# Second pair of delta-rule heads begun from keys and queries alone, values projected later

## The chip, the core and the metric

The kernel runs on one core of one Trainium2 chip and computes the whole model in one launch. The metric is the device time of one execution in microseconds, the median of several. TensorE (PE) multiplies matrices into PSUM; VectorE (DVE), ScalarE (ACT) and GpSimd (POOL) work beside it; SyncE (SP), ACT and POOL issue DMAs. Each engine runs its own instructions strictly in the order in which the program lists them and waits on semaphores for the others.

## The reference

Two residual layers on 512 tokens of width 1024, in float32. The even layer (the one that the change touches) projects the normed input h once and splits the columns: group A, four heads of a gated delta rule with short convolutions, and group B, four heads of differential attention. Both outputs go through one output projection. The odd layer is a forgetting attention. After each mixer follow a squared-ReLU MLP and a gated per-layer embedding. Of group A:

```python
qkv_a, z_a, b_a, a_a, q_b, k_b, v_b = split_cols(h @ w_in, EVEN_SPLITS)
qkv_a = silu(causal_conv(qkv_a, conv_w))           # width 4, per column
q_a, k_a = l2_norm(q_a), l2_norm(k_a);  beta = sigmoid(b_a);  g = -exp(a_log) * softplus(a_a + dt_bias)
# per head and chunk:
a_mat = tril(beta k k^T * decay, -1) + I           # needs keys, beta and g, no values
u, w  = solve(a_mat, [beta v, beta k exp(gc)])     # values enter only here
v_new = u - w S;  o = q_dec S + qk v_new;  S = S * g_last + k_dec^T v_new   # chunk after chunk
```

## The kernel before, in words

Every large product is made of three float32r products (high and low parts of weight and activation), so a weight half of 128 x 1024 is loaded by SP (`raw`), its high part is made by ACT and its low part by DVE (`whl`, three buffers, lines 146 and 149).

The even mixer is written as Python generators. A list of projections, `fill`, taken in the order of the string `ORDER` (line 72), gives TensorE its large products: `a0` to `a3` project one delta head's query and key columns each, `w0` and `w2` the values of two delta heads, `v0` and `v1` the values of the attention heads, `b0` to `b3` one attention head's query and key, and two more jobs project the gate z. Between them, `chains` (lines 676 and on) advance the heads themselves: each `yield n` says how much later on TensorE's own count of columns the next step may be written. What has been written is then ordered again per engine by the framework's scheduler, so that the place of an instruction follows from its estimate of when the inputs are there. On the chip that place is fixed.

A delta head (`gdn_head`, line 453) runs in these steps: the decays `et` from the gates (`decays`); key products `pg` and turned keys; a small column `lc` of each 16 x 16 diagonal block; the query-key product; squares of the keys `sqk` and queries `sqq`; the turned values `vb`. When both heads of a pair have their `lc`, `small_inverses` writes it to DRAM (`lsc`), copies it back to the rows of all blocks (`lb`) with DMAs issued by ACT, and makes 15 pairs of small steps on POOL (`xt`, `xc`, lines 446 and 448). Then POOL spreads the result to `x` (line 535), TensorE turns it to `z`, and three levels of products (`ub`, `yy`) build the inverse of each 128 x 128 block. At last comes the recurrence over four chunks: `rest`, `vn`, `state`, `u`, and a norm of the output (`sqo`, `sso`, `ro`, line 648).

Heads 0 and 1 are the first pair, 2 and 3 the second (`ABREAST` is 2). Heads 2 and 3 enter `gdn_head` at once but stay in its first loop (lines 454 and 455) until an earlier head is done and their values are projected:

```python
while len(done) < h + 1 - ABREAST or h >= ABREAST and h not in vts:
    yield 2.0
```

Tiles come from pools with a fixed number of buffers: `sp` (10) holds et, kd, u, x and z of the heads, `hl` (8) the split queries, keys and outputs and the attention values, `mm` (3) PSUM sums of projections, `ax` small PSUM products, `raw` and `whl` (3 each) the weights.

Of the kernel before, what the change touches and what calls it, by code (L numbers as in the profile page):

```python
# [10 lines left out]
F32 = mybir.dt.float32  # L11
F32R = mybir.dt.float32r
I32 = mybir.dt.int32
AF = mybir.ActivationFunctionType
ALU = mybir.AluOpType
# [3 lines left out]
P = 128  # L19
T = 512  # L20
NT = T // P
# [3 lines left out]
HA = 4  # L25
# [11 lines left out]
BASE = 16  # L37
# [31 lines left out]
LAT_A, LAT_B = 1.55, 1.7  # L69
W_G, W_B, W_T, W_V, W_Q = 10.0, 22.5, 20.0, 6.0, 3.6  # L70
Z_B, DSTEP = 3, 3.47
ORDER = "a0 a1 w0 v0 v1 b0 b1 a2 a3 w2 b2 b3"
ABREAST = 2
N_SP = 10
N_ST = 5
SRAW, SWHL, SA = 8, 3, 4
ORDER_MID, ORDER_END = (1, 5, 6, 7, 3, 4, 2), (1, 2, 5, 6, 3, 7, 4)
# [20 lines left out]
def trunk(ctx: ExitStack, tc: tile.TileContext, I, cst, out):  # L98
    nc = tc.nc
    V, S, G, PE = nc.vector, nc.scalar, nc.gpsimd, Tensor(tc)  # L100
# [13 lines left out]
    def aux():  # L114
        return pax.tile([P, T], F32, tag="ax", name="ax", bufs=2)
# [8 lines left out]
    def hl32():  # L124

        return hlp.tile([P, 2, T], F32, tag="hl", name="hl32")
# [12 lines left out]
    def v3(ap):  # L139
        return ap.rearrange("p (i c) -> p i c", c=P)  # L140
# [23 lines left out]
    ident, m_le, m_gt = (gen[:, j * P:(j + 1) * P] for j in range(3))  # L164
# [22 lines left out]
    def wsplit(raw, E=None):  # L187

        n = raw.shape[2]
        w = tile_of(whp, F32R, "whl", 2)[:, 0:8 * n].rearrange("p (j k c) -> p j k c", j=2, c=n)  # L190
        split(w[:, 0], w[:, 1], raw, E)
        return w

    def wload(src, spans, r0=0):
        return [wsplit(wraw(src, spans, r0 + half * 4 * P)) for half in range(2)]
# [126 lines left out]
    def even_mixer(act, first, wba):  # L322
        w_in = I["w_in_even"][0]
        with ExitStack() as es:
            gp = es.enter_context(tc.tile_pool(name="gp", bufs=1))
            def sp(name):
                return gp.tile([P, T], F32, tag="sp", name=name, bufs=N_SP)

            def st_(name):
                return gp.tile([P, T], F32, tag="st", name=name, bufs=N_ST)  # L330
# [66 lines left out]
            def conv_tile(ps, j, name):  # L397

                y = gp.tile([P, T], F32, tag="qkv", name=name, bufs=12)
                w = [cols[:, R_CONV + 12 * a + j:R_CONV + 12 * a + j + 1] for a in range(4)]  # L400
                S.activation(out=y, in_=ps, func=AF.Copy, scale=w[3])
                for a in (2, 1, 0):
                    d = 3 - a
                    V.scalar_tensor_tensor(out=y[:, d:], in0=ps[:, :T - d], scalar=w[a], in1=y[:, d:],
                                           op0=ALU.mult, op1=ALU.add)
                return y

            def silu(*tiles):
                for y in tiles:
                    S.activation(out=y, in_=y, func=AF.Silu)  # L410

            def hcol(name, h):
                return st[name][:, :, h]

            def bc(ap):
                return ap.broadcast_to([P, NT, P])
# [16 lines left out]
            def small_inverses(pair):  # L433

                lc, n = small_l[pair], 2 * NT
                lsc = dp.tile([P // BASE, BASE * n * BASE], F32, tag="lsc", name="lsc", bufs=1)
                nc.scalar.dma_start(lsc.rearrange("b (r n) -> b r n", r=BASE), lc.rearrange("p h i c -> p (h i c)"))
                lb = gp.tile([P, BASE, n, BASE], F32, tag="lb", name="lb", bufs=1)
                for a in range(P // BASE):
                    nc.scalar.dma_start(lb[a * BASE:(a + 1) * BASE].rearrange("p r i c -> p (r i c)"),  # L440
                                        lsc[a:a + 1, :].broadcast_to([BASE, BASE * n * BASE]))
                yield 10.0
                xc = small_w[pair].rearrange("p h i c -> p (h i) c")
                tmp = gp.tile([P, n, BASE], F32, tag="xt", name="xt", bufs=1)
                for c in range(BASE - 1, 0, -1):
                    G.tensor_tensor(out=tmp[:, :, 0:c], in0=lb[:, c, :, 0:c],
                                      in1=xc[:, :, c].broadcast_to([P, n, c]), op=ALU.mult)
                    G.tensor_tensor(out=xc[:, :, 0:c], in0=xc[:, :, 0:c], in1=tmp[:, :, 0:c], op=ALU.add)
                yield 10.0
                solved.append(pair)  # L450

            def gdn_head(h, qT, kT):
                while len(done) < h + 1 - ABREAST or h >= ABREAST and h not in vts:
                    yield 2.0
                if h >= ABREAST:
                    yield from decays(h)
                blk = [slice(i * P, (i + 1) * P) for i in range(NT)]

                pair, sub = h // 2, h % 2
# [3 lines left out]
                pk = aux()  # L463
                for i in range(NT):
                    PE.transpose(pk[:, blk[i]], kT[:, blk[i]], ident)
                sq, kk = st_("sqk"), gp.tile([P, 2, NT], F32, tag="kk", name="kk", bufs=ABREAST)
                for i in range(NT):
                    S.activation(out=sq[:, blk[i]], in_=pk[:, blk[i]], func=AF.Square, accum_out=kk[:, 0, i:i + 1])
                kd = sp("kd")
                S.activation(out=kd, in_=pk, func=AF.Copy)  # L470
                dg = st_("dg")
                V.tensor_tensor(out=v3(dg), in0=v3(pg), in1=mid(gm["minus_base"]), op=ALU.mult)
                second = pair in small_l
# [5 lines left out]
                while h not in decay or "ec" not in st:  # L479
# [13 lines left out]
                                in1=s.broadcast_to([P, NT, BASE]), op=ALU.mult)  # L493
# [9 lines left out]
                                op=ALU.mult)  # L503
# [4 lines left out]
                for i in range(NT):  # L508
                    PE.matmul(pq[:, blk[i]], lhsT=kT[:, blk[i]], rhs=qT[:, blk[i]], start=True, stop=True)
                V.tensor_tensor(out=et, in0=pq, in1=et, op=ALU.mult)  # L510
                G.tensor_tensor(out=v3(kd), in0=v3(kd), in1=bc(hcol("ekd", h)), op=ALU.mult)

                pq = aux()
                for i in range(NT):
# [1 line left out]
                sq, eq = st_("sqq"), kk[:, 1]  # L516
# [6 lines left out]
                vT = vts[h][0]  # L523
# [4 lines left out]
                V.tensor_tensor(out=v3(vb), in0=v3(pv), in1=bc(n2), op=ALU.mult)  # L528
                yield 2.0

                while pair not in solved:
                    yield 1.0
                x, xc = sp("x"), small_w[pair][:, sub]
                for i in range(NT):
                    G.tensor_tensor(out=x[:, blk[i]].rearrange("p (b c) -> p b c", c=BASE),
                                    in0=xc[:, i, :].unsqueeze(1).broadcast_to([P, P // BASE, BASE]),
                                    in1=gm["minus_base"].rearrange("p (b c) -> p b c", c=BASE), op=ALU.mult)
# [13 lines left out]
                for lv in LEVELS:  # L551
                    y, wide, full = st_("yy"), lv < 32, lv == P // 2
                    ub = u
                    if not full:
# [5 lines left out]
                        else:  # L560
                            for j in range(64 // lv):
                                c = slice((2 * j + 1) * lv, (2 * j + 2) * lv)
                                G.tensor_tensor(out=cut(ub, lv)[:, j::64 // lv], in0=v3(u)[:, :, c],
                                                in1=mu[:, c].unsqueeze(1).broadcast_to([P, NT, lv]), op=ALU.mult)
# [11 lines left out]
                    else:  # L576
                        for j in range(64 // lv):
                            S.activation(out=y[(2 * j + 1) * lv:(2 * j + 2) * lv, 0:T // 2],
                                         in_=py[j * lv:j * lv + lv, 0:T // 2], func=AF.Copy)
# [8 lines left out]
                    else:  # L588
                        for j in range(64 // lv):
                            zo = half(z[2 * j * lv:(2 * j + 1) * lv], lv, 1)[:, j::64 // lv]  # L590
                            V.tensor_tensor(out=zo, in0=zo, in1=cut(pt[j * lv:j * lv + lv], lv)[:, j::64 // lv],
                                            op=ALU.subtract)
# [11 lines left out]
                for n in range(NT):  # L604
                    vn = gp.tile([P, P], F32, tag="vn", name="vn", bufs=2 * ABREAST)
                    if n:
# [4 lines left out]
                                               in1=vb[:, blk[n]], op0=ALU.mult, op1=ALU.subtract)  # L611
# [7 lines left out]
                    if n < NT - 1:  # L619
                        ps = aux()  # L620
# [21 lines left out]
                sq = st_("sqo")  # L642
# [21 lines left out]
            def project_a(h):  # L664
                c = h * P
                tiles = []
                w = wload(w_in, [(C_Q + c, P), (C_K + c, P)]) if h else first
                pair = [acc(), acc()]
                steps = [gemm_steps(pair[m], w, m, act) for m in range(2)]
                if h == 0:  # L670
                    for _ in zip(*steps):
                        yield
                for m, ps in enumerate(pair):
                    yield from steps[m]
                    tiles.append(conv_tile(ps, 4 * m + h, "qk"[m] + "T"))
                    if h < ABREAST:
                        silu(tiles[-1])
                heads_a.append(tiles[0])
                late.extend(tiles if h >= ABREAST else [])
                spawn(gdn_head(h, *tiles), W_G)  # L680

            def values_a(h):
                w = wload(w_in, [(C_V + h * P, 2 * P)])
                for m in range(2):
                    ps = acc()
                    yield from gemm_steps(ps, w, m, act)
                    late.append(conv_tile(ps, 8 + h + m, "vT"))
                silu(*late)
                for m in range(2):
                    vts[h + m] = late[m - 2], PE.time + W_V * LAT_A  # L690
                late.clear()

            def project_b(h):
                c = h * P
# [54 lines left out]
            def spawn(g, after, lat=LAT_A):  # L749
                chains.append([PE.time + after * lat, g, lat])  # L750
# [3 lines left out]
            late, small_l, small_w, solved = [], {}, {}, []  # L754
            chains, done, done_b, started, heads_a, heads_o = [], [], [], [], [], [None] * (HA + HB)
            qks, vts, decay = {}, {}, {}
# [17 lines left out]
            while chains or fill:  # L774
                due = [c for c in chains if c[0] <= PE.time]
                free = [f for f in fill if f[0]()]
                if due:
                    c = min(due, key=lambda c: c[0])
# [615 lines left out]
    with tc.tile_pool(name="ip", bufs=1) as ip:  # L1394
# [18 lines left out]
        ps = acc()  # L1413
# [3 lines left out]
        for i in range(NT):  # L1417
# [3 lines left out]
            r, ok, ss = small(1, "rx"), small(1, "ok"), ssx[:, i:i + 1]  # L1421
# [6 lines left out]
            if i == 2:  # L1428
                ps = acc()
# [9 lines left out]
        act, _ = new_act()  # L1439
# [61 lines left out]
```

## Time and profile before

| | us |
|---|---|
| median of 3 runs | 1422.2 (1421.55 to 1423.59) |
| the profiled execution | 1421.96 |
| its span, first to last instruction | 1420.2 |
| TensorE busy / DVE / ACT / POOL | 1384.1 / 867.3 / 773.5 / 174.2 |
| mean granted TensorE clock | 0.989 |

The profile shows one execution. A line of a timeline gives the start, the busy time, the engine, the source line, the operation, output and inputs, the count and, in brackets, how long the engine was idle before and what ended that. PEclk is the share of the full TensorE clock that was granted. In groups, the busy time of a product can overlap the next one's, so what one costs is read from a run of them: so many products from one start to the next. The mixer covers about 20 to 322 us of the span.

### The profile page before, as it was taken

How to read it: one execution, taken by the hardware profiler on the slowest of the kernel's cores; microseconds unless marked ns; L12 is line 12 of the kernel's file. 1: busy time of each engine (PE TensorE's matmuls, PEld its weight loads, DVE VectorE, ACT ScalarE, POOL GpSimd, SP SyncE). 2: the span in 40 equal slices, each digit the busy share in tenths (PEclk: the TensorE clock that was granted, in tenths of full speed). 3: DMA queues.
4: the chain of work that ended last, by engine and by line, in shares of the span. 5: the costliest groups of instructions: out<-in, count | busy, mean ns of one | idle time of the engine just before them, and what ended most of it. 6: DMA issues, size and time to landing. Idle time of an engine off the chain costs nothing. (4 is left out here: it accounts for less than half of the span.)

```text
span 1420.2 us, 18495 instructions
## 1 busy us (share of the span) xinstructions
PE 1384.1 (97%) x6969; PEld 1152.2 (81%) x6969; DVE 867.3 (61%) x1535; ACT 773.5 (54%) x1304; POOL 174.2 (12%) x231
## 2 busy tenths in 40 slices
PE   8999987999999999999999999999999999999997
PEld 6887775777888888888878888888888888888887
DVE  6837786665465665657665746646646565655865
ACT  6746775663555564556534545535355555554643
POOL 1350056010110201101001000000011020101100
PEclk9999998999999999999999999999999999999999
DMA  6251213114954856566333443852295476756611
GB/s 179 79 106 46 60 31 77 45 55 168 250 135 136 176 154 160 140 159 129 93 72 60 60 89 60 79 97 90 89 270 135 132 153 174 159 143 146 132 60 60
DMA packets 134238, 164.61 MB, mean 116 GB/s; under 512 B 9650, under 2 KB 91396, under 8 KB 133892
## 3 DMA queue, kind: packets, MB, share of 16 engines
q1 hardware_dynamic: 113968, 123.82, 32.6%
q0 software_dynamic: 15360, 33.56, 13.8%
q10 hardware_dynamic: 4820, 6.05, 1.9%
q8 instruction: 55, 0.90, 0.3%
q14 instruction: 35, 0.29, 0.1%
HBM read 152.78 MB, written 2.23 MB: 109 GB/s over the span
## 5 line engine op out<-in xcount | busy, mean ns | idle before, releaser
L90 PE MATMUL mm<-act,whl 128*128 128x512 f32 (+1 forms) x2784 | 657.9, 389 | 2.6 <-DVE whl L149 1.9
L90 PEld LDWEIGHTS mm<-act,whl 128*128 128x128 f32 x2784 | 506.3, 190 | 103.0 <-DVE whl L149 3.2
L90 PE MATMUL ax<-swhl,sa 128*128 128x512 f32 x1344 | 314.0, 389 | 0.0
L90 PEld LDWEIGHTS ax<-swhl,sa 128*128 128x128 f32 x1344 | 252.1, 188 | 52.4
L149 DVE TENSOR_TENSOR whl<-raw,whl 128x1024 fp32r<-128x1024 f32 x139 | 170.6, 1228 | 167.5 <-ACT whl L146 164.7
L149 DVE TENSOR_TENSOR swhl<-sraw,swhl 128x1024 fp32r<-128x1024 f32 x112 | 136.9, 1222 | 124.4 <-ACT swhl L146 124.2
L146 ACT ACTIVATE whl<-raw 128x1024 fp32r<-128x1024 f32 (+1 forms) x140 | 147.9, 1057 | 54.5 <-PE mm L90 50.2
L146 ACT ACTIVATE swhl<-sraw 128x1024 fp32r<-128x1024 f32 x112 | 118.8, 1060 | 101.2 <-PE ax L90 86.7
L90 PE MATMUL mm<-whl,act 128*128 128x256 f32 (+2 forms) x720 | 108.0, 307 | 0.2 <-ACT act L146 0.2
L1261 ACT ACTIVATE r<-mm 128x512 f32<-128x512 f32 x64 | 38.2, 597 | 126.0 <-PE mm L90 125.9
L90 PEld LDWEIGHTS mm<-whl,act 128*128 128x128 f32 x720 | 97.0, 190 | 6.7 <-ACT act L146 0.7
L1165 POOL DMA_DIRECT2D sraw<-w_mlp_down x48 | 57.5, 1218 | 251.0 <-DVE swhl L149 115.6
L319 DVE TENSOR_TENSOR x_tok<-x_tok,ax 128x512 f32<-128x512 f32 x114 | 73.5, 681 | 10.8 <-PE ax L90 10.7
L90 PE MATMUL mm<-owhl,act 128*128 128x256 f32 (+1 forms) x336 | 57.9, 329 | 0.0
L90 PE MATMUL mm<-owhl,hl 128*128 128x512 f32 x228 | 54.8, 397 | 0.0
L90 PEld LDWEIGHTS mm<-owhl,act 128*128 128x128 f32 x336 | 49.6, 188 | 6.4
L312 POOL TENSOR_TENSOR rn<-tn,nhalf 128x1 f32<-128x1 f32 x12 | 6.6, 553 | 385.9 <-DVE tn L311 385.9
L1165 POOL DMA_DIRECT2D sraw<-sraw x16 | 14.6, 915 | 302.5 <-DVE swhl L149 276.2
L90 PEld LDWEIGHTS mm<-owhl,hl 128*128 128x128 f32 x228 | 42.4, 188 | 10.1
L1174 ACT ACTIVATE sraw<-sraw 128x1024 f32<-128x1024 f32 x32 | 33.8, 1058 | 27.0 <-DVE swhl L149 17.5
L146 ACT ACTIVATE act<-ax 128x512 fp32r<-128x512 f32 x40 | 22.4, 595 | 43.1 <-PE ax L94 42.9
L149 DVE TENSOR_TENSOR sa<-hl,sa 128x512 fp32r<-128x512 f32 x64 | 43.8, 685 | 0.0
(341 smaller groups left out, 1609.6 us busy)
## 6 DMA issues: line engine op xcount, KB each, us to landing
raw<-w_mlp_up SPq DMA_DIRECT2D x64, 512.0 KB, 4.3
sraw<-w_mlp_down SPq DMA_DIRECT2D x64, 512.0 KB, 3.9
sraw<-w_mlp_down POOLq DMA_DIRECT2D x48, 512.0 KB, 5.8
raw<-w_in_even SPq DMA_DIRECT2D x32, 256.0 KB, 3.5
sraw<-sraw POOLq DMA_DIRECT2D x16, 512.0 KB, 6.3
raw<-w_ple_gate SPq DMA_DIRECT2D x16, 512.0 KB, 4.9
raw<-w_in_odd SPq DMA_DIRECT2D x16, 512.0 KB, 5.2
raw<-w_in_odd SPq DMA_DIRECT2D x32, 256.0 KB, 6.6
```

What stands on the lines that cost most here:

```text
L90: return self.tc.nc.tensor.matmul(out, lhsT=lhsT, rhs=rhs, start=start, stop=stop, skip_group_check=onto)
L146: S.activation(out=hi, in_=src, func=AF.Copy)
L149: return (E or V).tensor_tensor(out=lo, in0=src, in1=hi.bitcast(F32), op=ALU.subtract)
L312: G.tensor_tensor(out=r, in0=t, in1=nhalf[:, 0:1], op=ALU.pow)
L319: V.tensor_tensor(out=x_tok[i][:, cs], in0=x_tok[i][:, cs], in1=ps, op=op)
L1165: G.dma_start(o, t, accum_op=ALU.add)
L1174: S.activation(out=t, in_=t, func=AF.Copy, scale=-1.0)
L1261: S.activation(out=r, in_=ps, func=AF.Relu)
```

## The change

Heads 2 and 3 no longer wait at the top. They are started when the last of the query and key projections is there, run through their steps up to the small inverses, and wait before `x` until the earlier head is done. Their decayed keys `kd`, which would hold a buffer all that time, are made after that wait from a second transpose of the keys, by DVE instead of ACT and POOL. In `ORDER`, `a2` and `a3` stand before the rest of the attention heads and `v1` after `w2`. The copies of `lc` lie in two tiles of the pool `hl` instead of one tile of their own, and there are two DMAs for each block row instead of one, each of half the size. `sp` gets 14 buffers, `kk` four.

```diff
-ORDER = "a0 a1 w0 v0 v1 b0 b1 a2 a3 w2 b2 b3"
+ORDER = "a0 a1 w0 v0 b0 a2 a3 b1 w2 v1 b2 b3"
-N_SP = 10
+N_SP = 14
...
-                lb = gp.tile([P, BASE, n, BASE], F32, tag="lb", name="lb", bufs=1)
+                lbs = [hl32().rearrange("p a (r i c) -> p (a r) i c", r=BASE // 4, c=BASE) for _ in range(2)]
+                part = BASE // 2 * n * BASE
                 for a in range(P // BASE):
-                    nc.scalar.dma_start(lb[a * BASE:(a + 1) * BASE].rearrange("p r i c -> p (r i c)"),
-                                        lsc[a:a + 1, :].broadcast_to([BASE, BASE * n * BASE]))
+                    for j, lb in enumerate(lbs):
+                        nc.scalar.dma_start(lb[a * BASE:(a + 1) * BASE].rearrange("p r i c -> p (r i c)"),
+                                            lsc[a:a + 1, j * part:(j + 1) * part].broadcast_to([BASE, part]))
...
             def gdn_head(h, qT, kT):
-                while len(done) < h + 1 - ABREAST or h >= ABREAST and h not in vts:
-                    yield 2.0
...
-                kd = sp("kd")
-                S.activation(out=kd, in_=pk, func=AF.Copy)
+                if h < ABREAST:
+                    kd = sp("kd")
+                    S.activation(out=kd, in_=pk, func=AF.Copy)
...
-                G.tensor_tensor(out=v3(kd), in0=v3(kd), in1=bc(hcol("ekd", h)), op=ALU.mult)
+                if h < ABREAST:
+                    G.tensor_tensor(out=v3(kd), in0=v3(kd), in1=bc(hcol("ekd", h)), op=ALU.mult)
...
-                while pair not in solved:
+                while pair not in solved or len(done) < h + 1 - ABREAST:
                     yield 1.0
+                if h >= ABREAST:
+                    kd, pk = sp("kd"), aux()
+                    for i in range(NT):
+                        PE.transpose(pk[:, blk[i]], kT[:, blk[i]], ident)
+                    V.tensor_tensor(out=v3(kd), in0=v3(pk), in1=bc(hcol("ekd", h)), op=ALU.mult)
...
-                late.extend(tiles if h >= ABREAST else [])
-                spawn(gdn_head(h, *tiles), W_G)
+                if h < ABREAST:
+                    spawn(gdn_head(h, *tiles), W_G)
+                else:
+                    late.append(tiles)
+                if h == HA - 1:
+                    silu(*(t for pair in late for t in pair))
+                    for j, pair in enumerate(late):
+                        spawn(gdn_head(ABREAST + j, *pair), W_G)
```

The order moves on TensorE, around the first pair's `x` (`gen` holds the identity, so these are transposes). Before, behind the rotary tables (`rope_w`), the products of v1 (128 x 256), b0 and b1 (128 x 512) and the first scores (`ax_1169`, ...) come first:

```order
L90 MATMUL mm<-whl,act 128x256 x30
L94 MATMUL ax<-gen,rope_w 128x128 x8
L90 MATMUL mm<-whl,act 128x256 x78
L90 MATMUL mm<-act,whl 128x512 x78
L90 MATMUL ax_1169<-hl 128x256
L90 MATMUL ax_1169<-kl,hl 128x256
L90 MATMUL ax_1180<-hl 128x256
L90 MATMUL ax_1180<-kl,hl 128x256
L90 MATMUL mm<-act,whl 128x512 x9
L90 MATMUL ax_1203<-hl 128x256
L90 MATMUL ax_1203<-kl,hl 128x256
L94 MATMUL ax<-gen,x 128x128 x4
```

Now the 128 x 512 products are those of a2 and b0, mixed, and then of a3:

```order
L90 MATMUL mm<-whl,act 128x256 x12
L90 MATMUL mm<-act,whl 128x512 x12
L94 MATMUL ax<-gen,rope_w 128x128 x8
L90 MATMUL mm<-act,whl 128x512 x38
L94 MATMUL ax<-gen,x 128x128 x2
L90 MATMUL mm<-act,whl 128x512 x58
L90 MATMUL ax_1085<-hl 128x256
L90 MATMUL ax_1085<-kl,hl 128x256
```

Two transposes of x stand 50 products behind v0, in front of every score; before, all of v1 and 87 products stood there.

On ACT, around the second pair's copies of `lc`. Before, rotary evictions (`rot`) and splits (`hl`, `whl`) of a later attention head are next to them:

```order
L437 DMA lsc<-lc 128x128
L518 ACTIVATE sqq,kk<-ax 128x128 x4
L146 ACTIVATE hl<-a 64x512
L702 ACTIVATE rot<-mm 32x512
L440 DMA lb<-lsc 16x2048 x8
L702 ACTIVATE rot<-mm 32x512 x2
L146 ACTIVATE whl<-raw 128x1024
```

Now these are the last two of 16 copies, which alternate between two tiles, and what stands behind them:

```order
L442 DMA hl_1741<-lsc 16x1024
L442 DMA hl_1742<-lsc 16x1024
L624 ACTIVATE vn<-ax 128x128
L930 ACTIVATE do<-ax_1800 128x128
L924 ACTIVATE at<-ax_1860 128x128
L652 ACTIVATE sqo,sso<-u 128x128
L401 ACTIVATE vT<-mm,cols 128x512
L640 ACTIVATE u<-ax,eg 128x128
L930 ACTIVATE do<-ax_1881 128x128
L410 ACT_TABLE_LOAD
L410 ACTIVATE vT<-vT 128x512
```

The copies have moved from beside a projection into the middle of the first pair's recurrence (`vn`, `u`) and of attention head b1 (`at`, `do`).

On TensorE, around the second pair's `x`. Before, it follows the scores of an attention head, with 5 products between:

```order
L90 MATMUL ax_2349<-hl 128x256
L90 MATMUL ax_2349<-kl,hl 128x256
L90 MATMUL mm<-act,whl 128x512 x5
L94 MATMUL ax<-gen,x 128x128 x3
L94 MATMUL ax_2433<-gen,p_2312 128x128
L94 MATMUL ax<-gen,x 128x128
L90 MATMUL ax<-x,ub 128x64 x4
```

Now it follows the turned outputs `u` of the first pair and the turned values and keys of the second:

```order
L94 MATMUL ax<-gen,u 128x128 x4
L94 MATMUL ax<-gen,vT 128x128 x4
L94 MATMUL ax_2178<-gen,p_1891 128x128 x3
L94 MATMUL ax<-gen,vT 128x128 x4
L90 MATMUL mm<-act,whl 128x512
L90 MATMUL ax_2213<-hl,at 128x128 x3
L94 MATMUL ax<-gen,kT 128x128 x4
L90 MATMUL mm<-act,whl 128x512
L94 MATMUL ax<-gen,kT 128x128 x4
L90 MATMUL mm<-act,whl 128x512 x10
L94 MATMUL ax<-gen,x 128x128 x4
```

What made x wait there, the pair's first part, has moved in front of the end of the first pair.

## Rows read from the trace of the kernel before

**Rows 1.** Page, busy us (share of the span) and instructions of each engine.
```profile
PE 1384.1 (97%) x6969; PEld 1152.2 (81%) x6969; DVE 867.3 (61%) x1535; ACT 773.5 (54%) x1304; POOL 174.2 (12%) x231
```
**Rows 2.** Stretch: us, PE, PEld, DVE, ACT, POOL busy, PEclk, DMA share, GB/s.
```profile
240.00:260.00 20.00, 18.16 (x78) 14.52 (x78) 9.93 (x27) 10.65 (x25) 6.72 (x13) 0.61 0.01 2
```
**Rows 3.** Waits of PE, 20 to 340 us: total, times, longest.
```profile
PE ax L94 <- POOL x L535: 7.1, 2, 6.8
PE ax L94 <- DVE u L649: 3.3, 3, 2.1
PE ax L90 <- DVE hl L720: 2.8, 1, 2.8
PE ax L94 <- DVE lc L502: 1.6, 1, 1.6
...
PE mm L90 <- DVE whl L149: 1.1, 1, 1.1
```
**Rows 4.** Timeline of PE around the second pair's x.
```profile
215.79 10.96 PE L90 MATMUL mm<-act,whl 128*128 128x512 f32 x47
...
241.45 0.48 PE L94 MATMUL ax<-gen,x 128*128 128x128 f32 x1 [6.75 <-POOL x L535]
...
251.66 2.05 PE L90 MATMUL mm<-act,whl 128*128 128x512 f32 x4
```
**Rows 5.** Timeline of POOL, second pair.
```profile
225.73 0.54 POOL L446 TENSOR_TENSOR xt<-lb,xc 128x120 f32<-128x120 f32 x1 [2.18 <-DMA lb<-lsc]
...
240.95 3.83 POOL L535 TENSOR_TENSOR x<-xc,gmask 128x128 f32<-128x128 f32 x8
```
**Rows 6.** Timeline of ACT: both sets of copies, and what follows them.
```profile
71.77 0.33 ACTq L440 DMA_DIRECT2D lb<-lsc  x1
...
72.62 2.79 ACTq L440 DMA_DIRECT2D lb<-lsc  x6
75.45 0.38 ACT L662 ACTIVATE hl<-mm 128x256 f32<-128x256 f32 x1 [2.92 <-PE mm L90]
...
214.69 0.31 ACTq L440 DMA_DIRECT2D lb<-lsc  x1
...
215.97 4.97 ACTq L440 DMA_DIRECT2D lb<-lsc  x5
220.98 1.19 ACT L702 ACTIVATE rot<-mm 32x512 f32<-32x512 f32 x2 [4.69 <-DMA raw<-w_in_even]
```
**Rows 7.** Timeline of PE: v0's end, rotary tables, first scores of b0.
```profile
73.21 3.84 PE L90 MATMUL mm<-whl,act 128*128 128x256 f32 x30
76.89 1.04 PE L94 MATMUL ax<-gen,rope_w 128*128 128x128 f32 x8
...
109.23 0.55 PE L90 MATMUL ax<-hl 128*128 128x256 f32 x1 [2.81 <-DVE hl L720]
...
111.25 4.21 PE L90 MATMUL mm<-act,whl 128*128 128x512 f32 x9
```
**Rows 8.** Timeline of POOL, first pair.
```profile
81.83 0.40 POOL L446 TENSOR_TENSOR xt<-lb,xc 128x120 f32<-128x120 f32 x1 [7.90 <-DMA lb<-lsc]
...
87.45 1.19 POOL L446 TENSOR_TENSOR xt<-lb,xc 128x72 f32<-128x72 f32 x1
88.72 1.40 POOL L448 TENSOR_TENSOR xc<-xc,xt 128x72 f32<-128x72 f32 x1
...
95.70 3.41 POOL L535 TENSOR_TENSOR x<-xc,gmask 128x128 f32<-128x128 f32 x8
```
**Rows 9.** Copies of lc (line 440), issue to landing.
```profile
DMA to landing us min/median/max: 3.7/5.7/7.3
```
**Rows 10.** Write of lc to lsc (line 437), issue to landing.
```profile
DMA to landing us min/median/max: 1.5/1.5/1.5
```
**Rows 11.** Timeline of DVE beside the first pair's chain.
```profile
87.03 1.42 DVE L149 TENSOR_TENSOR whl<-raw,whl 128x1024 fp32r<-128x1024 f32 x1 [6.21 <-ACT whl L146]
```
**Rows 12.** Group: table loads of ACT, 20 to 340 us; busy, mean ns.
```profile
L410 ACT ACT_TABLE_LOAD x10 | 12.8, 1283 | 4.3 <-DVE qT L404 2.0 <-DVE kT L404 1.1 <-DVE mx L891 0.5
```

More of the change, by code (lines that the diff above doesn't have):

```diff
@@ L445, in small_inverses @@
                 for c in range(BASE - 1, 0, -1):
-                    G.tensor_tensor(out=tmp[:, :, 0:c], in0=lb[:, c, :, 0:c],
+                    G.tensor_tensor(out=tmp[:, :, 0:c], in0=lbs[c // 8][:, c % 8, :, 0:c],
                                       in1=xc[:, :, c].broadcast_to([P, n, c]), op=ALU.mult)
@@ L465, in gdn_head @@
                     PE.transpose(pk[:, blk[i]], kT[:, blk[i]], ident)
-                sq, kk = st_("sqk"), gp.tile([P, 2, NT], F32, tag="kk", name="kk", bufs=ABREAST)
+                sq, kk = st_("sqk"), gp.tile([P, 2, NT], F32, tag="kk", name="kk", bufs=HA)
                 for i in range(NT):
                     S.activation(out=sq[:, blk[i]], in_=pk[:, blk[i]], func=AF.Square, accum_out=kk[:, 0, i:i + 1])
-                kd = sp("kd")
-                S.activation(out=kd, in_=pk, func=AF.Copy)
+                if h < ABREAST:
+                    kd = sp("kd")
+                    S.activation(out=kd, in_=pk, func=AF.Copy)
                 dg = st_("dg")
@@ L678, in project_a @@
                 heads_a.append(tiles[0])
-                late.extend(tiles if h >= ABREAST else [])
-                spawn(gdn_head(h, *tiles), W_G)
+                if h < ABREAST:
[6 more added lines that the diff above has]
+                        spawn(gdn_head(ABREAST + j, *pair), W_G)
             def values_a(h):
                 w = wload(w_in, [(C_V + h * P, 2 * P)])
+                tiles = []
                 for m in range(2):
@@ L686, in values_a @@
                     yield from gemm_steps(ps, w, m, act)
-                    late.append(conv_tile(ps, 8 + h + m, "vT"))
-                silu(*late)
+                    tiles.append(conv_tile(ps, 8 + h + m, "vT"))
+                silu(*tiles)
                 for m in range(2):
-                    vts[h + m] = late[m - 2], PE.time + W_V * LAT_A
-                late.clear()
+                    vts[h + m] = tiles[m], PE.time + W_V * LAT_A
             def project_b(h):
```

## The prediction

> **What bounds the kernel now.** I read the busy line of the page first [rows 1]: TensorE is busy for 97% of the span and no other engine for more than 61%, so a change pays only by taking idle time or half-clock time off TensorE. The stretches of 20 us [rows 2] put the largest such loss of the even mixer into 240 to 260, right behind a wait of TensorE (18.16 of 20 us busy, but at a clock of 0.61). The waits of TensorE over the mixer [rows 3] name the causes: POOL's x tiles (7.1 us in two waits), the key halves of head b0 (2.8), the scaled outputs u (3.3) a column lc of the second pair (1.6) and a weight's low half (1.1).
>
> The largest of them in order of time [rows 4]: the last product ends at 234.7, the transposes of x start at 241.45 after 6.75 us of idle time, a second one follows after 0.38, and then products of 512 columns run at 0.51 us each (2.05 for 4), where 47 of them took 10.96 before, 0.233 each. That is the lower of the two clock levels, 1.2 instead of 2.4 GHz, and it holds until about 256. POOL shows why x is late [rows 5]: the 30 steps of the second pair's small inverses begin at 225.73, when the copies of lc have landed, and the x tiles follow them at 240.95.
>
> **The change, part by part.** The sum is made against the profiled execution, 1421.96 us (span 1420.2 and 1.8 around it), 0.2 under the median of 1422.2.
>
> *Removed: the wait for the second pair's x.* The pair's decays, key products, inverses and copies are issued before the first pair ends; on POOL the 30 steps now stand ahead of the first pair's output norm, and on TensorE x comes behind both u, the values and the keys of the first pair's successors, with 10 products in front. Gone: 6.75 + 0.38 = 7.1 us, and the lower clock of 241.45 to 256, 14.6 us that cost about half, 7.0. Gain 14.1. The wait for lc (1.6) [rows 3] and 0.2 beside it leave their place too, 1.8; but the same column has to be made in the new place between denser steps, and I put 1.0 back.
>
> *New wait 1: the first pair's copies and x.* Copying lc to the rows of the inverse takes 16 DMA issues of half the size instead of 8. The issues hold ACT: six took 2.79, 0.455 apart with their gaps, and the next activation began at 75.45, right behind the last [rows 6]. So 16 from 71.77 end at 79.05. Behind them in ACT's order stand two evictions of v0 (0.7), and then the second weight half of a2 (1.06), whose low part takes DVE 1.23 more. TensorE is there earlier: v0 ends at 74.7 (12 products into the 30 of 3.84 us) and the 8 rotary transposes take 0.8 [rows 7]; with a2's first 12 products (2.8) it arrives at 78.3 and waits 2.6 for the high and 1.0 for the low half. The first half of b0 follows on ACT after the two rotary tables (1.1): high at 83.1, low at 84.3, waits of 0.5 and 0.55. Then 22 products (5.1) and 6 (1.4). The three weight buffers then hold both halves of a2 and one of b0, so b0's second half can be split only when the first is read out, at 89.4; high at 90.6, and TensorE stands at the first transposes of x at 91.7.
>
> Those were 50 products into b0 and a2 moved ahead of where they stood: x is asked for 24 us earlier than in the kernel before (115.91). POOL is no faster. In the kernel before its steps begin at 81.83, x at 95.70, 13.87 later, with the first two of x's eight blocks 0.85 after that [rows 8]. The last of 16 copies is issued at 78.6, and the quickest copy in the trace landed 3.7 us after its issue [rows 9], so 82.3; x is ready at 97.0 and TensorE waits 5.3. Bounds: 80.1 for the landing if it takes 1.5, as the 64 KB of lsc did [rows 10]; 85.9 at the slowest copy, 7.3. For the clock after it I have two rows: 2.81 us of waiting were followed by 9 products in 4.21 us instead of 2.1 and by four score products 0.8 longer, so 2.9 [rows 7]; 6.75 us were followed by a loss of 7.0. Between them, 5.3 costs 5.5. Sum of the new losses from 74.7 on: 2.6 + 1.0 + 0.5 + 0.55 + 5.3 + 5.5 = 15.4. What they take the place of: 1.1 (a weight of b1) and 2.8 [rows 3] and 2.9, 6.8. Net 8.6, between 5 and 14.
>
> A rule weighed here: two steps of the chain, 0.36 us otherwise, took 1.19 and 1.40, and DVE's low-part subtraction of a weight, 87.03 to 88.45, stands right beside the first [rows 8, 11]. The Trainium skill (GPSIMD Engine Reference, Specifications) says that GpSimd shares its SBUF interface with VectorE and is slowed by VectorE instructions with two SBUF inputs; the trace agrees, at about 0.9 us per subtraction. In my walk two subtractions fall into the chain, as before, so the 13.87 stand; a third would make it 0.9 longer and the sum about 1.8 larger.
>
> *New wait 2: the second pair's copies stand in front of the first pair's recurrence.* On ACT the 16 issues now come straight ahead of vn (the new values of head 1), an eviction do and an at of b1; before, only rotary evictions stood behind them. Call T the end of the query transposes of head 3. ACT needs 1.2 for the squares, and lsc lands 1.5 after an issue that waits for lc: copies from T+1.8 to T+9.1, vn, do and at until T+10.1. TensorE has 13 products of 512 columns (3.0), 24 of 256 (0.123 each, 2.95) and small ones, 7.3 in all, and then needs at: 2.8 of waiting. Behind at, ACT has six activations of 0.3 to 0.7, a table load of 1.28 [rows 12] and v1's second weight half (1.06): T+15.8, its low part T+17.0; TensorE would have wanted it at T+10.3. So 6.6 in all, the clock's fall lying inside the second wait. Bounds: with issuing at no price ACT would be done at T+9.7, loss 0; at the dearest rate in the trace, five issues in 4.97 us with ACT idle for 4.69 [rows 6], 16 take 15.9 and the loss is 15.
>
> The Trainium skill (DMA: Bandwidth & Descriptors, Issuing engines are not separate DMA queues) says that the time to initiate a DMA is usually small beside the DMA itself. By that rule this term would be nil; [rows 6] show 0.44 us per issue on an engine on the path, and I stay with the rows.
>
> *Small parts.* The keys of heads 2 and 3 are transposed twice: 8 transposes, 0.7 us, on TensorE's path. Their decayed copy moves from ACT (0.6) and POOL (1.05) to DVE (0.7) per head; neither waits there. More buffers for sp and kk cost no time. The wait for u (3.3) stays: in the new order the last scores leave about 4.6 us where 7 are needed.
>
> Sum: 8.6 + 6.6 + 0.7 + 1.0 - 14.1 - 1.8 = +1.0. **Forecast 1423 us**, own range 1418 to 1428: one new wait of 14 us in two pieces eats what the old one gives.
>
> **The rivals.**
> *A, the new waits mostly hide.* If the copies land at 81 and TensorE reaches x two us later than I think (its own clock falls after the first 2.6), the x wait is 2 and its clock loss 2.5: 6 less; the second wait then starts from a TensorE that is later on other counts, 3 less. 1423 - 10 = 1413. For it: a TensorE that is held once lets ACT and DVE catch up, and 120 to 180 has hardly a wait. Against it: both waits are fixed by an order on ACT and POOL.
> *B, issuing costs next to nothing* (the skill's rule above): wait 2 goes, wait 1 stays as POOL sets it. 1423 - 6.6 = 1416.5. Against it: 4.69 us of ACT idle.
> *C, slower: the second set of copies issues as slowly as it did before.* Place: ACT, between the squares of head 3 and vn. That set's 8 issues took 6.25 (214.69 to 220.94), 0.78 each; 16 take 12.5, 5.2 more than summed, and the longer wait draws about 2 more of low clock: 1430. It decides from 0.6 us per issue on (2.4 us more). For it: weights are on their way at both times. Against it: the first set did not slow down.
> *D, the change doesn't do what it says.* The second chain ends at T + 1.8 + 11 + 13.9 = T+26.7, and the first pair's norm, queued behind it on POOL, is due at about T+28. If the copies land 6 us later, the norm and both u wait: 1429, and the early start buys no earlier end.
>
> **How the numbers follow.** Forecast 0.45, A 0.22, B 0.07, C 0.20, D 0.06. Within 0.2% (2.8 us, about what a measurement tells from no change) means 1419.4 to 1425.0. The forecast's own spread gives 0.09 faster, 0.22 same, 0.14 slower; A is all faster, B 0.06 of 0.07; C 0.18 slower, 0.02 same; D slower. Faster 0.37, same 0.25, slower 0.38. The range of 8 in 10 reaches from A's time to just past C's: 1412 to 1432.
>
> **What would show it.** Right: no wait for x near the second pair's start and a clock of 1.00 there; a wait of 4 to 6 us for POOL's x near 92 to 97 with a clock below 0.8 behind it; 16 issues of 0.45 on ACT twice, and about 6 us of TensorE waiting for at and for a weight near the second set. Wrong: x of the first pair in time, or TensorE busy through the second set (A, B); issues of 0.8 us (C); u waiting for POOL's norm (D).

## The result, and the profile after

The changed kernel takes 1429.6 us (median of four runs, 1428.08 to 1431.24) where the kernel before takes 1422.2: a ratio of 1.0051, 95% interval 1.0033 to 1.0068, so about 7 us slower. The profiled execution took 1429.14, with a span of 1427.3.

The busy line of the page, against [rows 1]: TensorE is busy 6.5 us longer, of which the eight more transposes account for 0.7.

```profile
PE 1390.6 (97%) x6977; PEld 1155.2 (81%) x6977; DVE 867.3 (61%) x1537; ACT 766.0 (54%) x1297; POOL 171.7 (12%) x229
```

Stretches of 20 us of the changed kernel, columns as in [rows 2]:

```profile
80.00:100.00 20.00, 15.72 (x50) 11.44 (x51) 6.20 (x6) 4.41 (x6) 14.69 (x38) 0.78 0.31 81
180.00:200.00 20.00, 18.09 (x103) 15.54 (x102) 9.86 (x25) 13.01 (x26) 10.21 (x24) 0.83 0.35 91
240.00:260.00 20.00, 19.92 (x125) 15.01 (x123) 14.98 (x51) 13.70 (x38) 2.56 (x2) 1.00 0.10 29
340.00:360.00 20.00, 17.06 (x70) 13.74 (x69) 10.74 (x22) 4.42 (x11) 1.67 (x3) 0.83 0.14 45
```

The hole of [rows 2] is gone: 19.92 us busy at full clock. Three others have opened, the last outside the mixer. The waits of TensorE from 20 to 345 us, against [rows 3]:

```profile
PE ax L94 <- DVE do L955: 4.5, 2, 2.5
PE ax L94 <- DVE spare L315: 2.9, 1, 2.9
PE ax L94 <- POOL x L542: 2.9, 1, 2.9
PE mm L90 <- ACT whl L146: 2.4, 1, 2.4
PE mm L90 <- DVE whl L149: 1.8, 3, 0.9
PE ax L94 <- ACT et L429: 1.4, 1, 1.4
...
PE ax L90 <- DVE hl L733: 1.2, 1, 1.2
PE ax L90 <- ACT vn L624: 0.9, 2, 0.5
```

The second pair's x is no longer in the list (the 2.9 are the first pair's), and neither are lc and the scaled outputs u. New are `whl` at 81, x at 96, `vn` at 186, both `do`, and `spare`, the normed tokens behind the output projection.

TensorE's timeline, at the first new waits (against [rows 7]), at the end of the mixer and in the output projection:

```profile
80.79 0.72 PE L90 MATMUL mm<-act,whl 128*128 128x512 f32 x1 [2.38 <-ACT whl L146]
82.05 11.46 PE L90 MATMUL mm<-act,whl 128*128 128x512 f32 x37 [0.54 <-DVE whl L149]
96.37 0.74 PE L94 MATMUL ax<-gen,x 128*128 128x128 f32 x2 [2.86 <-POOL x L542]
...
317.86 0.66 PE L94 MATMUL ax<-gen,do 128*128 128x128 f32 x4 [1.97 <-DVE do L955]
...
324.52 4.36 PE L90 MATMUL mm<-owhl,hl 128*128 128x512 f32 x18
...
344.43 1.97 PE L94 MATMUL ax<-gen,spare 128*128 128x128 f32 x8 [2.94 <-DVE spare L315]
346.05 7.88 PE L90 MATMUL mm<-owhl,hl 128*128 128x512 f32 x24
```

The kernel before in the output projection, TensorE and then ACT:

```profile
322.44 4.36 PE L90 MATMUL mm<-owhl,hl 128*128 128x512 f32 x18
...
340.21 1.09 PE L94 MATMUL ax<-gen,spare 128*128 128x128 f32 x8 [0.80 <-DVE spare L315]
341.06 5.86 PE L90 MATMUL mm<-owhl,hl 128*128 128x512 f32 x24
...
314.12 0.67 ACT L949 ACTIVATE hl<-ax,dnorm 128x512 fp32r<-128x512 f32 x1
...
335.19 1.06 ACT L146 ACTIVATE whl<-raw 128x1024 fp32r<-128x1024 f32 x1 [1.62 <-DMA raw<-w_mlp_up]
```

The 37 products behind the first waits take 0.31 us each on average, where the 47 of [rows 4] took 0.233: after 2.9 us of waiting the granted clock of 80 to 100 is 0.78. The first product with `owhl` (the later five of the eight weight halves of the output projection) divides the time: before, it starts at 322.44 and 1097.8 us of span are left; here at 324.52, with 1102.8 left. So the mixer is 2.1 us longer, and what follows it 5.0, though the change touches no line there. ACT, against [rows 6], and in the output projection:

```profile
72.53 6.56 ACTq L442 DMA_DIRECT2D hl<-lsc  x14
79.14 0.66 ACT L669 ACTIVATE hl<-mm 128x256 f32<-128x256 f32 x2 [6.71 <-DMA hl<-lsc]
...
178.51 6.86 ACTq L442 DMA_DIRECT2D hl<-lsc  x14
185.47 0.28 ACT L624 ACTIVATE vn<-ax 128x128 f32<-128x128 f32 x1 [6.86 <-DMA hl<-lsc]
...
318.55 0.69 ACT L962 ACTIVATE hl<-ax,dnorm 128x512 fp32r<-128x512 f32 x1 [5.71 <-PE ax L94]
...
339.35 1.06 ACT L146 ACTIVATE whl<-raw 128x1024 fp32r<-128x1024 f32 x1 [2.76 <-DMA raw<-w_mlp_up]
340.31 0.62 ACT L304 ACTIVATE sqf<-x_tok 128x512 f32<-128x512 f32 x1
```

Both sets of 16 hold ACT for about 7 us. At the end, attention head b3's output is split at 318.55 (before, 314.12); the first splits of the output weights queue behind it on ACT, free their `raw` buffers 3.75 later, and so the MLP's third weight half is there only at 339.35 (before, 335.19). The squares of the first token tile stand right behind that split on ACT, as they did before, and `spare` waits for them.

POOL, against [rows 8]: the chain starts and ends where it was expected. (The last copy is issued at 78.66 and copies take up to 3.5 us to land, so its landing is as late as the DVE instruction that the row names.)

```profile
82.19 0.40 POOL L448 TENSOR_TENSOR xt<-hl,xc 128x120 f32<-128x120 f32 x1 [8.35 <-DVE whl L149]
...
95.86 3.36 POOL L542 TENSOR_TENSOR x<-xc,gmask 128x128 f32<-128x128 f32 x8
```

### The profile page after: what moved, and what is told of

Its sections match the earlier page's. It is cut to its first block, busy times and chain, and to the rows that moved or that the text cites. A ratio compares the mean times of both kernels' runs of the same rounds, so it can differ in the third digit from the quotient of the medians.

```text
span 1427.3 us, 18533 instructions
## 1 busy us (share of the span) xinstructions
PE 1390.6 (97%) x6977; PEld 1155.2 (81%) x6977; DVE 867.3 (61%) x1537; ACT 766.0 (54%) x1297; POOL 171.7 (12%) x229
## 4 chain that ended last, share of the span: by engine, by line
PE 84%; issue 4%; DVE 3%; ACT 3%; DMA 2%; POOL 2%; ACTq 1%; SPq 0%; POOLq 0%; DVEq 0%
PE mm L90 53%; PE ax L90 28%; PE ax L94 3%; ACTq L442 1%; ACT rot L715 1%; DMA raw<-w_out_even 1%; DMA sraw<-w_mlp_down 1%; POOL xt L448 0%; DMA raw<-w_ple_gate 0%; DVE whl L149 0%; DMA raw<-w_mlp_up 0%; POOL xc L450 0%; DVE owhl L149 0%; ACT whl L146 0%; DVE spare L315 0%
## 5 line engine op out<-in xcount | busy, mean ns | idle before, releaser
L90 PE MATMUL mm<-whl,act 128*128 128x256 f32 (+2 forms) x720 | 112.8, 311 | 0.6 <-DVE whl L149 0.4
```

The costliest lines, as they stand in the source:

```text
L90: return self.tc.nc.tensor.matmul(out, lhsT=lhsT, rhs=rhs, start=start, stop=stop, skip_group_check=onto)
```

## The experiments

Ratios are to the kernel before on the same chip, with their 95% interval. "x wait" is a wait of TensorE for POOL's x.

**e1: 8 issues instead of 16, the order unchanged.**

```diff
-for a in range(8):      # 16 partitions each
-    lsc[a:a + 1, part].broadcast_to([16, part])
+for a in range(0, 8, 2):  # 32 partitions each
+    lsc[a:a + 2, part].unsqueeze(1).broadcast_to([2, 16, part])
```

> The changed kernel with 8 DMAs instead of 16 for each set of copies of lc (32 partitions each instead of 16, the same bytes into the same two tiles); the order on every engine is otherwise the same. Theory (the issues hold ScalarE, 0.47 us each): both sets take 3.5 us instead of 6.9; TensorE's waits for the halves of a2 near 81 (2.4 and 0.5) go, the first pair's x comes about 3.5 us earlier but TensorE too, so its wait stays near 3; the waits of 1.8 us behind the second set (186 to 193) go with half of the low clock there. 1422 to 1425. Rival (POOL and the landing of the copies set both waits, issuing is cheap): the bigger copies land later, x comes when it did, no more than 2 us are gained: 1428 to 1430.

1449.8 us, 1.0197 (1.0177 to 1.0218): both expectations missed. ACT, POOL and PE of e1:

```profile
72.56 0.61 ACTq L442 DMA_DIRECT2D hl<-lsc  x1
...
76.42 2.76 ACTq L442 DMA_DIRECT2D hl<-lsc  x1
...
98.65 0.40 POOL L448 TENSOR_TENSOR xt<-hl,xc 128x120 f32<-128x120 f32 x1 [24.70 <-DMA raw<-w_in_even]
...
110.94 0.89 PE L94 MATMUL ax<-gen,x 128*128 128x128 f32 x2 [17.99 <-POOL x L542]
```

Seven issues of 32 rows hold ACT for 6.6 us, as long as 14 of 16 rows, but not evenly: six take 0.61 us each and the last 2.76 (3.02 in the second set). What held the last is not shown. And the chain on POOL, which waits for the copies, starts 16 us later. The same four microseconds of the changed kernel, and then of e1 (DMA share and GB/s at the end):

```profile
76.00:80.00 4.00, 2.41 (x15) 1.87 (x13) 0.00 (x0) 0.86 (x3) 0.00 (x0) 1.00 0.88 136
```

```profile
76.00:80.00 4.00, 2.53 (x16) 1.96 (x14) 0.00 (x0) 0.77 (x3) 0.00 (x0) 1.00 0.12 47
```

The share falls from 0.88 to 0.12, about two of the sixteen DMA engines. The Trainium skill (DMA: Bandwidth & Descriptors, Why a DMA increments its semaphore by 16 and not by 1) says that a DMA is spread over the largest number of engines, up to 16, that divides the slowest dimension (other than 1) of both its sides; here these are 2 and 32, so 2 engines. The trace agrees. So e1 does not settle what the issues cost; it shows that a late x costs TensorE nearly its full lateness (the x wait grows from 2.86 to 17.99).

**e2: attention last in the output projection.**

```diff
-w, pairs = I["w_out_even"][0], (0, 2, 3, 1)
+w, pairs = I["w_out_even"][0], (0, 2, 1, 3)
```

> The changed kernel with the output projection's inner products taken in the order of head pairs 0, 2, 1, 3 instead of 0, 2, 3, 1: the second attention pair last instead of the second delta pair. Only the stretch from 310 to 350 us changes. Theory (the mixer now ends with attention head b3, and the squares of the first token tile stand on ScalarE behind the split of a weight that lands late): the wait for do (1.97 near 317.9) goes, the squares stand in front of that split, so the wait for spare (2.94 near 344.4) falls below 1 and TensorE's clock stays at 1.00 from 340 to 360: 1423 to 1425, 4 to 6 less than the changed kernel. Rival (the output projection is paced by the landing of its weights and by the eviction of b3): TensorE comes to spare 2 us earlier and waits as much longer: 1428 to 1430.

1424.1 us, 1.0018 (1.0002 to 1.0033), against 1.0051: about 4.7 us back, as the theory said, but not wholly as it said. The wait for `do` fell to 1.09, that for `spare` only to 2.51, and the clock from 340 to 360 was 0.91. The squares stand behind the second weight half now and are done by 334.4, but the third half still holds `spare`: on DVE its low part stands in front of the norm's factor `rn`.

```profile
337.44 1.23 DVE L149 TENSOR_TENSOR whl<-raw,whl 128x1024 fp32r<-128x1024 f32 x1 [1.95 <-ACT whl L146]
338.59 0.15 DVE L313 TENSOR_TENSOR rn<-rn,okn 128x1 f32<-128x1 f32 x1
```

From the first `owhl` on 1100.8 us are left, 2.0 fewer than in the changed kernel. Another 3.0 us of its profile's gain were there before any instruction differed (the transposes of `do` ahead of b3's start at 301.58 instead of 304.58), with the same waits at a higher clock. So the edit itself is worth 3 to 5.

**e3: the old sequence of projections, 16 copies.**

```diff
-ORDER = "a0 a1 w0 v0 b0 a2 a3 b1 w2 v1 b2 b3"
+ORDER = "a0 a1 w0 v0 v1 b0 b1 a2 a3 w2 b2 b3"
```

> The changed kernel with the sequence of projections of the kernel before (v1, b0 and b1 ahead of a2 and a3); the early start of the second pair, the 16 copies, the later keys and the buffers stay. Theory (the loss is in the sequence, which asks for the first pair's x 24 us earlier than POOL has it and lets attention end last; the early start by itself gains): no wait for x near 96, the clock 1.00 from 80 to 100; no wait for x of the second pair near 240; the attention heads end as early as in the kernel before: 1409 to 1416. Rival (the second set of 16 copies on ScalarE costs as much wherever it falls, and the delta chain ends the mixer again): 1420 to 1425.

1422.0 us, 1.0001 (0.9984 to 1.0019): the rival's time. So the new sequence costs about 7 us (1.0051 against 1.0001), but without it the gain is still missing. PE of e3, behind the second set of copies:

```profile
225.61 0.47 PE L90 MATMUL mm<-act,whl 128*128 128x512 f32 x1 [2.72 <-DVE a L718]
229.36 1.65 PE L90 MATMUL mm<-act,whl 128*128 128x512 f32 x3 [3.28 <-DVE whl L149]
...
242.11 0.33 PE L94 MATMUL ax<-gen,x 128*128 128x128 f32 x1 [0.62 <-POOL x L542]
```

The x wait of 6.75 us is down to 0.62, and 6.0 us of waiting stand 13 us ahead of it, since the rotary evictions and a split had stood behind 16 issues on ACT (209.4 to 219.4, with a standstill of 2.8 in them, see e4). Ahead of v1, the first set costs 2.5 and 0.4.

**e4: the kernel before, with 16 copies.** The edit is the hunk of `lb` and `lbs` alone.

> The kernel before with the copies of lc as 16 DMAs of half size into two tiles of the split queries' pool, in place of 8 into a tile of their own; nothing else. Theory (each issue holds ScalarE 0.45 us): the first set ends 3.6 us later, covered by the products of v1 but for 1 us; the second set ends 3.5 to 6 us later and the second pair's x with it, a wait of 10 to 12 instead of 6.75 us near 240: 1426 to 1431. Rival (the issues hide behind TensorE's products, and smaller copies land sooner): 1421 to 1423.

1426.7 us, 1.0038 (1.0023 to 1.0053). ACT and PE of e4:

```profile
213.73 2.33 ACTq L442 DMA_DIRECT2D hl<-lsc  x5
217.79 4.08 ACTq L442 DMA_DIRECT2D hl<-lsc  x9
...
239.23 1.71 PE L94 MATMUL ax<-gen,x 128*128 128x128 f32 x4 [8.34 <-POOL x L537]
```

The x wait is 8.3 (10 to 12 expected), with 2.5 in front of v1 and 2.6 near 225. The halved copies, with their move into `hl`, cost 5 us. The issues are no slower here than in the first set, 0.47 us from one to the next, but one of them stands for 1.7 us, until a weight half that SP had issued at 212.59 has landed 5.2 us later; in the trace the two use the same semaphore. The second set of the kernel before, ACT:

```profile
217.38 0.44 ACTq L440 DMA_DIRECT2D lb<-lsc  x1
...
220.63 0.31 ACTq L440 DMA_DIRECT2D lb<-lsc  x1
```

That is the same standstill: the last issue waited 2.8 us for a weight half issued at 214.36 that took 6.2 us to land. So the 0.78 us of rival C, and the prediction's dearest rate of five issues in 4.97 us [rows 6], were one wait and not slow issues.

**e5: the copies issued by SyncE.**

```diff
-nc.scalar.dma_start(lb[a * BASE:(a + 1) * BASE]
+nc.sync.dma_start(lb[a * BASE:(a + 1) * BASE]
```

> The changed kernel with all 16 copies of each set issued by SyncE instead of ScalarE; TensorE's order then has the first pair's x behind the first scores instead of in front of them. Theory (the issues hurt because they hold ScalarE): no wait for the halves of a2 near 81, for x near 96 and for vn, u, at near 186; the clock 1.00 from 80 to 100; the end of the mixer as in the changed kernel: 1414 to 1420. Rival (SyncE is held for 7 us as ScalarE was, and the weights queued behind come late): waits for whl of 3 us and more behind each set: 1426 to 1431.

1423.7 us, 1.0013 (1.0004 to 1.0021): between the two. The waits for a2's halves and for the first x are gone and the clock is 1.00 from 80 to 100; but this order waits 3.3 us for a key eviction at 101 and 3.2 for the second pair's x at 217.8, and `do` and `spare` stay (4.2 and 2.0). ACT's hold was real; taking it away gave 5.4 us back (1.0051 to 1.0013), and the order that came with it brought two new waits of 6.5.

**e6: the old sequence and the old 8 copies; what is left is the early start.**

```diff
-ORDER = "a0 a1 w0 v0 b0 a2 a3 b1 w2 v1 b2 b3"
+ORDER = "a0 a1 w0 v0 v1 b0 b1 a2 a3 w2 b2 b3"
-N_SP = 14
+N_SP = 10
-lbs = [hl32() ... for _ in range(2)]          # 16 x 4 KB rows, 16 issues
+lb = gp.tile([P, BASE, n, BASE], tag="lb", bufs=1)   # 16 x 8 KB rows, 8 issues
```

> The changed kernel with the sequence of projections of the kernel before and the copies as there: 8 DMAs of 16 x 8 KB into a tile of their own (sp with 10 buffers, which frees its space). What is left of the change is the early start and the later keys. Theory (with that sequence the 16 issues cost 2.8 us in front of v1 and 6 us and low clock near 225, as e3 showed; the early start takes the second pair's x wait away): waits near 80 and 225 below 1.5 us, x wait below 1.5: 1408 to 1415. Rival (the early start moves the copies so little, 209 instead of 215, that the time is that of the kernel before): 1419 to 1423.

1414.1 us, 0.9949 (0.9937 to 0.9961): faster than both kernels. The waits and stretches of e6:

```profile
PE ax L94 <- DVE u L654: 3.1, 3, 2.1
...
PE mm L90 <- DVE whl L149: 2.4, 2, 1.5
...
PE mm L90 <- DVE a L716: 1.0, 1, 1.0
```

```profile
220.00:240.00 20.00, 17.40 (x66) 12.46 (x64) 11.78 (x27) 10.45 (x19) 16.78 (x36) 0.83 0.27 75
240.00:260.00 20.00, 19.89 (x105) 14.78 (x104) 17.02 (x47) 15.61 (x32) 4.79 (x8) 1.00 0.16 53
```

No x wait, full clock behind it; 2.5 us of waits and a clock of 0.83 remain near 225, behind the 8 issues. e3 has the same sequence with 16 copies in other tiles and is 7.4 us slower (1.0001 to 0.9949).

**e7: v1 first, then the early pair.** e6 with `ORDER = "a0 a1 w0 v0 v1 b0 a2 a3 b1 w2 b2 b3"`.

> As e6, but the sequence is a0 a1 w0 v0 v1 b0 a2 a3 b1 w2 b2 b3: v1 stands in front, as in the kernel before, and covers the first pair's chain, and a2 and a3 stand before b1, as in the changed kernel. Theory (early x and 16 issues were the cost, the place of a2 and a3 was not): no x wait of either pair, second set of copies well ahead of its need; the end set by attention head b3 with 3 to 5 us around spare: 1411 to 1417. Rival (issues in the middle of the recurrence cost as in the changed kernel, attention's lateness costs the rest): 1420 to 1426.

1424.3 us, 1.0024 (1.0014 to 1.0034): the rival's time, by a cause neither had. POOL, DVE and PE of e7:

```profile
205.39 0.40 POOL L446 TENSOR_TENSOR xt<-lb,xc 128x120 f32<-128x120 f32 x1 [7.93 <-DMA lb<-lsc]
...
218.60 0.92 DVE L718 TENSOR_TENSOR a<-a,rot 128x512 f32<-128x512 f32 x1 [7.66 <-POOL rot L717]
...
220.77 1.11 PE L94 MATMUL ax<-gen,kT 128*128 128x128 f32 x4 [8.83 <-DVE mx L902]
```

A rotary product of an attention head stands behind the 30 steps on POOL; DVE waits for it, and TensorE for what stands behind it on DVE. The steps themselves were late: the 8 copies took from 190.9 to 201.0, with weights on their way again.

**e8: e7 with the edit of e2.**

> e7 with the output projection's inner products in the order of head pairs 0, 2, 1, 3, as in e2. Theory: what stands before the wait for do covers it, and the squares are not behind the third weight; 3 to 5 us less than e7: 1407 to 1413. Rival (TensorE comes to spare sooner and waits there): the same as e7 within 2 us.

1421.3 us, 1.0008 (0.9995 to 1.0022): about 2.3 us less than e7, but the intervals overlap, so theory (3 to 5) and rival (within 2) are not told apart; `do` 1.1, `spare` 1.0, the wait of 8.6 as before.

**e9: e6, the second set issued by SyncE** (`(nc.sync if pair else nc.scalar)`).

> e6 with the second pair's 8 copies issued by SyncE instead of ScalarE. Theory (what is left near 225, 1.0 and 1.5 us of waiting and a clock of 0.83 behind them, comes from 8 issues that hold ScalarE in front of the rotary evictions): both waits go and the clock is 1.00 from 220 to 240; 1409 to 1412. Rival (the weight that SyncE brings next comes as much later): 1413 to 1416.

1421.1 us, 1.0000 (0.9991 to 1.0009): 7 us worse than e6. The two waits are gone, but the edit moved the order on all engines: 2.8 us for a split query at 222, 4.1 for an attention row at 253, a clock of 0.83, 0.82 and 0.76 from 220 to 280. Inconclusive for its question.

**e10: the changed kernel again.**

> The changed kernel once more, unaltered, on the chip of e9 and e11. Theory (waits are fixed by the order, the granted clock behind them is not): the same waits as in its first profile within 0.3 us each, a clock that differs in some stretches between 60 and 240, and a median of 1427 to 1431. Rival (its first runs lay high): 1421 to 1425.

1426.9 us, 1.0051 (1.0038 to 1.0064): the same ratio, the median just below the theory's range. Of the larger waits most agree within 0.3 us (2.39, 2.58, 2.49, 1.99; `spare` 3.56 and a weight at 190, 1.09 instead of 0.40, do not); the clock from 160 to 180 is 1.00 instead of 0.91, from 180 to 200 it is 0.91 instead of 0.83. The first `owhl` product is at 321.31 of a span of 1424.3: the mixer 1.1 us shorter than before, what follows 5.2 longer.

**e11 and e12: the rotary product on VectorE**, in e8 and in e6.

```diff
-G.tensor_tensor(out=rot, in0=rot, in1=sinr, op=ALU.mult)
+V.tensor_tensor(out=rot, in0=rot, in1=sinr, op=ALU.mult)
```

> e8 with the rotary product rot x sinr (line 717) made by VectorE instead of GpSimd. Theory (the 8.6 us of waiting near 220 in e7 and e8 come from that product standing behind the second pair's 30 steps in GpSimd's queue; the attention chain waits for it): that wait falls below 2 and the clock from 200 to 240 is 1.00: 1409 to 1414. Rival (the wait is for the second pair's x, which the chain of 30 steps sets anyway): a wait of 5 to 8 for x in its place: 1419 to 1422.

e11: 1418.2 us, 0.9977 (0.9967 to 0.9987), 4 less than e8 by the ratios, just under the rival's range. The wait of 8.6 is gone, and an x wait of 5.2 stands in its place: both theories had a part of it.

> e6 with the rotary product rot x sinr (line 717) made by VectorE instead of GpSimd. Theory (in e6 too that product can stand behind the 30 steps and hold an attention head's queries; the wait of 1.0 for a and of 1.5 for a weight near 225 come of it): both are shorter and the clock is 1.00 from 220 to 240: 1408 to 1412. Rival (there they come from the 8 issues on ScalarE, and VectorE has 1.3 us more per half head): 1413 to 1418.

e12: 1414.9 us, 0.9963 (0.9950 to 0.9976): e6's time within their intervals, the rival's. The waits near 225 stay (1.04 and 1.35, clock 0.83). Its mixer ends 4.7 us before e6's (first `owhl` at 309.98 instead of 314.68), and the output projection takes it back. ACT of e12, in front of a wait of 3.59 for `spare` at 330.54:

```profile
325.51 1.06 ACT L146 ACTIVATE whl<-raw 128x1024 fp32r<-128x1024 f32 x1 [2.52 <-DMA raw<-w_mlp_up]
326.48 0.62 ACT L304 ACTIVATE sqf<-x_tok 128x512 f32<-128x512 f32 x1
```

It is the picture of the changed kernel's end, in another order: squares behind a weight that lands late.

## Why the forecast came out 6.6 us low

The time of 1429.6 lies in the prediction's range of 8 in 10 (1412 to 1432), but 1.6 us outside the forecast's own (1418 to 1428). That it is also the time of rivals C (1430) and D (1429) is chance: neither happened. By steps:

- *The second pair's x wait goes (14.1), the wait for lc too (1.8).* Right at its place: no x wait, 19.92 us busy at 1.00.
- *New wait 1 (net 8.6, bounds 5 to 14).* The mechanism was right, the size just under its lower bound. The halves of a2 cost 2.38 and 0.54 (2.6 and 1.0 forecast), the chain started at 82.19 (82.3), x was there at 96.4 (97.0). But TensorE was late too: its clock had fallen behind the first wait, as rival A had it (whose two gains, 6 and 3, make 1414 and not 1413), and it reached x at 93.5, not 91.7. The x wait was 2.86 instead of 5.3. With 0.88 for a weight at 110.33 and a clock of 0.78 and 0.97 over 80 to 120 (20 x 0.22 + 20 x 0.03 = 5.0) that is 11.7 gross instead of 15.4, net 4.9.
- *New wait 2 (6.6).* The copies held ACT from 177.7 to 185.4, 0.47 us an issue, and `vn` stood behind them, as forecast. TensorE paid in five short waits (0.54, 0.19, 0.25, 0.44, 0.40), 1.8 us, and a clock of 0.83 over 180 to 200 (20 x 0.17 = 3.4): 5.2. (The forecast's 8.6 and 6.6 make 15.2, not the 14 us of its last line.) Rival B is refuted: `vn` stood behind 6.86 us of issues, and 8 more issues in each set cost 5 and 7 us (e4; e3 against e6). The Trainium skill (DMA: Bandwidth & Descriptors, Issuing engines are not separate DMA queues) says that the time to initiate a DMA is usually small beside the DMA itself. For one copy the trace agrees (0.43 us, against a median of 3.0 from issue to landing); that the term would be nil does not follow, since sixteen such issues stand in front of ACT's own work. C's 0.78 us did not come (no weight was on its way, see e4), D did not happen (the norm `ro` ran at 206.2, its u did not wait).
- *"The wait for u (3.3) stays", and the sum ends with the mixer.* This step failed. u was ready (no wait for it is left); instead TensorE waits 2.5 and 2.0 for `do` of attention, whose projections the new sequence puts later, and 1.4 and 1.2 near 155 to 160. The sum had the mixer at +1.0, and it was +2.1 and, in e10, -1.1, but that is partly luck: with the two new waits at 4.9 and 5.2 the same sum gives -4.1, the waits it had wrong (`do` 3.5 more than before, 2.6 near 155 to 160, 3.3 less for u) bring it to -1.3, and what the other 3 us of this profile are is not shown. And it had nothing for the 20 us behind the mixer: the late end of b3 delays the output weights, these the MLP's, and with them the squares on ACT. `spare` waits 2.94 instead of 0.80, and at the fallen clock the next 24 products take 7.88 instead of 5.86: 5.0 and 5.2 us in the two profiles, the larger part of the 7.

By whole kernels, one part after the other: the early start alone -7.3 us (e6, 0.0051 of 1422), 16 copies instead of 8 +7.4 (e3 against e6), the new sequence +7.1 (1.0051 against e3). The three add up to the whole by construction, and each difference of two ratios carries some 3 us; the copies' price has a second witness in e4 (5 us). I had put nearly all of the price on the copies and the early x, and on the sequence's far end nothing. What stays open: e3 and e6 also differ in where the copies lie and in buffers, and the framework's order moves with every edit, so that only e1, e2 and e8 against e7 (these two up to the output projection) hold the order fixed. The new sequence with the old 8 copies was not run, since e1 lost the spread over the DMA engines.

## What to carry to other kernels

A step that is moved takes its DMA issues with it: price them on the engine that issues them, issue by issue (0.47 us each here), and look at what stands behind them and at what an issue itself may have to wait for. A wait that is removed shows only where the time was lost, so follow the new order to the first point behind the stage where all weights and buffers must be back, here the output projection, and ask there which chain now ends last. When a change of several parts moves little, run each part alone: here, in the order e6, e3, changed kernel, one part gave 7 us and two took 7 each.

## What the runs showed of the hardware

- Issue time on ACT: an issue of 16 rows took 0.43 us, of 8 KB rows (kernel before) as of 4 KB rows (changed kernel), 0.47 from one to the next; one of 32 rows of 4 KB took 0.61 (e1). In the second sets of the kernel before, e3 and e4 one issue stood 2.8, 2.8 and 1.7 us, until a weight that SP had issued was there.
- Two DMA steps can carry the same bytes over all or few engines, by the shape of the access alone (0.88 or 0.12 of the sixteen DMA engines' time, changed kernel and e1).
- The granted clock behind the same waits differs between executions of one program (1.00 instead of 0.91 from 160 to 180 in e10). e8's twelve runs lie between 1417.75 and 1428.42 us; the six with a mean clock of 0.992 and more took 1417.75 to 1420.84, the six with less 1421.75 to 1428.42.
